# Gate and up chunks by seven products over all of K, interleaved with the down projection, in a two-layer encoder trunk

## The chip, the core and the metric

The kernel runs on one core of a Trainium2 chip. The metric is device time in microseconds (us) of one execution. TensorE (PE) multiplies, VectorE (DVE) and ScalarE (ACT) work on elements, GpSimd (POOL) and SyncE (SP) issue DMAs here, and 16 DMA engines carry the data. A trace is the record of one execution, every instruction with its start and duration.

## The reference

Two layers over 256 tokens of width 2048: an input projection, attention and retention heads, an output projection, then a gated feed-forward part, each followed by a layer norm. What matters here is the feed-forward part:

```
D_MODEL = 2048; SEQ = 256; DEPTH = 2
D_FF = -(-(8 * D_MODEL) // (3 * 256)) * 256          # 5632
...
f = (jax.nn.silu(x @ w_gate[l]) * (x @ w_up[l])) @ w_down[l]
x = layer_norm(ALPHA * x + f, ln2_g[l], ln2_b[l])
```

All of it is float32, and the weights are read once from the chip's memory (HBM).

## The kernel before

**Three products for one.** A float32 operand is split in two: `hi`, a copy rounded to the matmul's format (fp32r), and `lo`, what the copy left out. A product is then hi·hi + hi·lo + lo·hi, three TensorE instructions (lines 252 to 254, 819 to 821). `split` (L263) makes the two: ACT casts `hi` (L264), then DVE subtracts (L265).

**Weight units.** The weights come in units, in the order of the list `UNITS`. A plain unit (`std`) is one block of 512 rows and 512 columns, 128x2048 in the core's memory, 1 MB. The class `Weights` runs three steps ahead: `_load` issues the DMA on SP (L162), `_prep` splits a unit (L183 to L206), `get` hands it to the products, and `done` (L240) preps the unit three further on. There are three `hi` and three `lo` buffers. So the cast of a unit can't start until TensorE is done with the unit three before it.

**Chunks.** 11 chunks of 512 columns make up the 5632 columns of gate and up. Chunk 0 is plain. In chunks 1 to 10, gate and up of the same columns, two halves of the tokens and two blocks of rows form a 2 by 2 matrix product, done with seven block products in place of eight. The blocks are 11 and 21 (gate, upper and lower rows) and 12 and 22 (up). Three products take a block as it is (B11, B21, B22), four take a sum: T1 = 11 + 12, T2 = T1 + 22, T4 = T2 + 21, T3 = 12 + 22. T1, T2 and T4 are made in place in the buffer of block 11, so each sum waits until the unit before it in that buffer is split. Before, a sum is made by DVE (L201), only T3 by a DMA that adds as it writes (L199, issued by POOL). The matching forms of the input, s1 to s4, are made once per layer (`s_sums`, `s_turn`). This covers 1024 of the 2048 rows; the other rows run as four plain units (sg2, sg3, su2, su3: gate and up).

**Order.** A chunk's units are B11, sg2, T1, B21, T2, sg3, T3, T4, su2, B22, su3. A product of one form has 12 matmuls of 512 columns, a plain unit has 24. The products go to the banks X, Q, W, Y, Z and R of PSUM (the tiles sX, sQ, ...), and eight DVE steps of 512 columns and three ACT steps join them into h. `h_flush` transposes h and splits it for the down projection. After chunks 0 to 2, 3 to 5, 6 and 7, and 8 to 10 (`FF_PARTS`) the down projection runs over those chunks: one unit of 24 matmuls of 512 columns per chunk and per quarter of the 2048 output columns (banks db), then two adds to the residual (L707).

Tile, the layer in which the kernel is written, schedules each engine's instructions by its own cost model when the program is built. Every engine then runs its list in that order.

Of the kernel before, what the change touches and what calls it, by code (L numbers as in the profile page):

```python
# [10 lines left out]
F32 = mybir.dt.float32  # L11
# [17 lines left out]
FF_PARTS = ((0, 3), (3, 6), (6, 8), (8, 11))  # L29
STRASSEN_ADD_BY_DMA = ("T3",)  # L30
# [14 lines left out]
def weight_plan():  # L45
# [9 lines left out]
    def strassen(l, c):  # L55
        b = {}
        for i in ("11", "12", "22", "21"):
            b[i] = add("w_gate" if i[1] == "1" else "w_up", l, 512 * (int(i[0]) - 1), 4, 512 * c, 512)
        for kind in ("B11", "sg2", "T1", "B21", "T2", "sg3", "T3", "T4", "su2", "B22", "su3"):
            if kind[0] == "s":  # L60
                block("w_gate" if kind[1] == "g" else "w_up", l, 512 * int(kind[2]), 4, 512 * c, 512)
            else:
                units.append((kind, b))

    for l in range(DEPTH):
# [25 lines left out]
        for f0, f1 in FF_PARTS:  # L91
            for c in range(f0, f1):
                if c == 0:
                    for name in ("w_gate", "w_up"):
                        for u in range(4):
                            block(name, l, 512 * u, 4, 512 * c, 512)
                else:
                    strassen(l, c)
            for n in range(4):
                for c in range(f0, f1):  # L100
                    block("w_down", l, 512 * c, 4, 512 * n, 512)
# [6 lines left out]
def shift(b):  # L108
    name, _, _, _, c0, ncol = PLAN[b]
    if name == "w_in" and ncol == 128:  # L110
        return 16
    if name == "w_uq" and c0 < 1024 or name == "w_ukv" and c0 < 1024:
        return 48
    return 0
# [9 lines left out]
def trunk(ctx: ExitStack, tc: tile.TileContext, x, pos, w, lnp, cols, eye, consts, out):  # L124
# [26 lines left out]
    class Weights:  # L151
# [26 lines left out]
        def _prep(self):  # L178
# [7 lines left out]
            if kind == "std":  # L186
                n = SIZES[b]
                raw = self.raw.pop(b)
                o = shift(b)
                for a, e in ((0, n // 2), (n // 2, n)):  # L190
                    split(hi[:, o + a:o + e], lo[:, o + a:o + e], raw[:, a:e])
            else:
                r = {j: self.raw.get(b[j]) for j in b}
                into, frm = {"B11": ("11", None), "B21": ("21", None), "B22": ("22", None), "T1": ("11", "12"),
                             "T2": ("11", "22"), "T4": ("11", "21"), "T3": ("12", "22")}[kind]
                if frm is not None:
                    if kind in STRASSEN_ADD_BY_DMA:
                        j = b[frm]
                        G.dma_start(r[into], w[OFFS[j]:OFFS[j + 1]].rearrange("(p n) -> p n", p=P), accum_op=ALU.add)  # L199
                    else:  # L200
# [27 lines left out]
        def get(self, m=1):  # L228
            r = []
            for _ in range(m):  # L230
# [3 lines left out]
                n, ncol, o = (SIZES[b], PLAN[b][5], shift(b)) if kind == "std" else (2048, 512, 0)  # L234
# [200 lines left out]
    for l in range(DEPTH):  # L435
# [330 lines left out]
        def s_sums():  # L766
            x_ = lambda t, c: res[:, t, 512 * c:512 * (c + 1)]
            sforms.extend(vt512(f"sf{i}") for i in range(4))
            s1, s2, s3, s4 = sforms
            V.tensor_tensor(s1, x_(1, 0), x_(1, 1), ALU.subtract)  # L770
            V.tensor_tensor(s2, x_(0, 0), s1, ALU.subtract)
            V.tensor_tensor(s3, x_(1, 0), x_(0, 0), ALU.subtract)
            V.tensor_tensor(s4, x_(0, 1), s2, ALU.subtract)

        def s_turn(u):
            for i in ((), (0, 1), (2,), (3,))[u]:
                pt = bank("pts")
                for j in range(4):
                    PE.transpose(pt[:, j * P:(j + 1) * P], sforms[i][:, j * P:(j + 1) * P], ident)
                split(sfh[:, i, :, :], sfl[:, i, :, :], pt.rearrange("p (j t) -> p j t", j=4))  # L780

        hprev = []

        def h_flush(hTh, hTl, f0):
            while hprev:
                t, c, hh = hprev.pop(0)
# [3 lines left out]
                k0 = 4 * (c - f0)  # L790
                split(hTh[:, k0:k0 + 4, t * P:(t + 1) * P], hTl[:, k0:k0 + 4, t * P:(t + 1) * P],
                      pt.rearrange("p (j t) -> p j t", j=4))

        def plain_group(c, flush):
            gb = [bank(f"gb{t}") for t in range(2)]
            chunk_head(gb, 512, 4, xTh, xTl, s_sums)
# [5 lines left out]
            flush()  # L802
            ub = [bank(f"ub{t}") for t in range(2)]
            chunk_plain(ub, 512, 4, xTh, xTl, 0, then=s_turn)
            for t in range(2):
                V.tensor_tensor(sg[t], sg[t], ub[t], ALU.mult)
                hprev.append((t, c, sg[t]))

        def strassen_group(c, flush):
            x11 = (xTh[:, 0:4, 0:P], xTl[:, 0:4, 0:P])  # L810
            x12 = (xTh[:, 4:8, 0:P], xTl[:, 4:8, 0:P])
            x22 = (xTh[:, 4:8, P:S], xTl[:, 4:8, P:S])
            s1, s2, s3, s4 = ((sfh[:, i], sfl[:, i]) for i in range(4))

            def mm(ps, unit, st, first=False):
                wh, wl = unit
                for k in range(4):
                    a, b = st[0][:, k, :], st[1][:, k, :]
                    PE.matmul(ps, a, wh[:, k, :], start=first and k == 0, stop=False, skip_group_check=True)  # L819
                    PE.matmul(ps, a, wl[:, k, :], start=False, stop=False, skip_group_check=True)  # L820
                    PE.matmul(ps, b, wh[:, k, :], start=False, stop=k == 3, skip_group_check=True)  # L821

            def xs(t, u):
                return (xTh[:, 4 * u:4 * u + 4, t * P:(t + 1) * P], xTl[:, 4 * u:4 * u + 4, t * P:(t + 1) * P])

            bX = bank("sX")
            (unit,) = W.get()
            mm(bX, unit, x11, True)
            v2 = vt512("v2")
            A.copy(v2, bX)  # L830
            W.done()
            bQ = bank("sQ")
            (unit,) = W.get()
            mm(bQ, unit, xs(1, 2), True)
            mm(bX, unit, xs(0, 2))
            W.done()
            flush()
            bW = bank("sW")
            (unit,) = W.get()
            mm(bW, unit, s1, True)  # L840
            W.done()
            (unit,) = W.get()
            mm(bX, unit, x12)
            W.done()
            bY = bank("sY")
            (unit,) = W.get()
            mm(bY, unit, s2, True)
            V.tensor_tensor(v2, bY, v2, ALU.subtract)
            W.done()
            (unit,) = W.get()  # L850
            mm(bX, unit, xs(0, 3))
            sg = vt512("sg")
            A.activation(sg, bX, AF.Silu)
            mm(bQ, unit, xs(1, 3))
            W.done()
            bZ = bank("sZ")
            (unit,) = W.get()
            mm(bZ, unit, s3, True)
            v3, v5 = vt512("v3"), vt512("v5")
            V.tensor_tensor(v3, bZ, v2, ALU.add)  # L860
            V.tensor_tensor(v5, bW, v3, ALU.add)
            W.done()
            (unit,) = W.get()
            mm(bQ, unit, x22)
            V.tensor_tensor(v3, bQ, v3, ALU.subtract)
            A.activation(v3, v3, AF.Silu)
            W.done()
            bR = bank("sR")
            (unit,) = W.get()
            mm(bR, unit, xs(1, 2), True)  # L870
            mm(bW, unit, xs(0, 2))
            W.done()
            (unit,) = W.get()
            mm(bW, unit, s4)
            W.done()
            (unit,) = W.get()
            mm(bW, unit, xs(0, 3))
            V.tensor_tensor(v2, bW, v2, ALU.add)
            V.tensor_tensor(v2, v2, sg, ALU.mult)
            mm(bR, unit, xs(1, 3))  # L880
            V.tensor_tensor(v5, bR, v5, ALU.add)
            V.tensor_tensor(v5, v5, v3, ALU.mult)
            W.done()
            hprev.append((0, c, v2))
            hprev.append((1, c, v5))
# [139 lines left out]
```

## Time and profile before

| | |
|---|---|
| device time, median of 3 | 2193.23 us (2192.56 to 2194.4) |
| the profiled execution's own time | 2195.18 us |
| its span, first to last instruction | 2193.4 us |
| TensorE busy | 2160.7 us (99%) |
| VectorE, ScalarE busy | 1590.7 us (73%), 1025.1 us (47%) |
| mean granted TensorE clock | 0.997 of full speed |

Busy time of an engine is the union of its instructions' spans. Matmuls overlap in the pipeline, so what one costs is the distance from its start to the next one's start, and not its duration in a row. The view of waits names, for each pause of an engine, who ended it.

### The profile page before, as it was taken

What the parts mean: (1) busy time and instruction counts of PE and PEld (TensorE: products, weight loads), DVE (VectorE), ACT (ScalarE), POOL (GpSimd) and SP (SyncE); (2) the same over time, 40 slices, a digit from 0 to 9 for tenths busy, and PEclk for the clock granted to TensorE, in tenths of its full rate; (3) what the DMA queues carried; (4) which work ended last, traced back from release to release, by engine and by line L of the source; (5) the groups of instructions that cost most, each with busy time, mean ns of one, the idle gap of its engine ahead of it and who ended that gap; (6) DMA issues with size and microseconds to landing.
All of it is one profiled execution on the core that took longest, in us unless ns stands there. A gap on an engine that the chain in (4) does not pass through costs nothing. (4 is left out here: it accounts for less than half of the span.)

```text
span 2193.4 us, 26857 instructions
## 1 busy us (share of the span) xinstructions
PE 2160.7 (99%) x11084; PEld 1839.4 (84%) x11084; DVE 1590.7 (73%) x1695; ACT 1025.1 (47%) x1089; POOL 35.5 (2%) x46
## 2 busy tenths in 40 slices
PE   7999999999999999999999999999999999999998
PEld 5988988788888888888889899878888888888886
DVE  8565675887698578788675656667966885877976
ACT  4554333555455345455344543335544553545552
POOL 0000000000000000000000000000000000000000
PEclk9999999999999999999999999999999999999999
DMA  7544555566567557475555444555665765666653
GB/s 258 208 156 152 175 194 190 211 211 230 173 224 257 206 196 245 163 254 203 189 185 184 154 156 172 211 192 192 219 241 177 246 235 173 206 249 211 211 211 115
DMA packets 63467, 440.70 MB, mean 201 GB/s; under 512 B 7408, under 2 KB 7664, under 8 KB 11504
## 3 DMA queue, kind: packets, MB, share of 16 engines
q1 hardware_dynamic: 60320, 417.94, 52.3%
q0 software_dynamic: 2880, 20.97, 5.2%
q8 instruction: 87, 1.43, 0.3%
q14 instruction: 36, 0.29, 0.0%
q10 hardware_dynamic: 144, 0.07, 0.0%
HBM read 436.85 MB, written 2.10 MB: 200 GB/s over the span
## 5 line engine op out<-in xcount | busy, mean ns | idle before, releaser
L264 ACT CAST hi<-raw 128x1024 fp32r<-128x1024 f32 (+3 forms) x754 | 875.5, 1201 | 981.1 <-PE db L254 294.0
L265 DVE TENSOR_TENSOR lo<-raw,hi 128x1024 fp32r<-128x1024 f32 (+3 forms) x754 | 1033.5, 1407 | 410.6 <-ACT hi L264 408.8
L252 PE MATMUL db<-hi,hTh 128*128 128x512 f32 x704 | 276.0, 392 | 0.0
L253 PE MATMUL db<-lo,hTh 128*128 128x512 f32 x704 | 274.1, 389 | 0.0
L254 PE MATMUL db<-hi,hTl 128*128 128x512 f32 x704 | 271.5, 389 | 0.0
L252 PEld LDWEIGHTS db<-hi,hTh 128*128 128x128 f32 x704 | 132.2, 188 | 30.1 <-ACT hTh L264 3.8
L254 PEld LDWEIGHTS db<-hi,hTl 128*128 128x128 f32 x704 | 132.1, 188 | 28.0
L253 PEld LDWEIGHTS db<-lo,hTh 128*128 128x128 f32 x704 | 132.2, 188 | 26.6
L259 PE MATMUL prq<-xTh,hi 128*128 128x256 f32 x512 | 144.3, 282 | 0.0
L260 PE MATMUL prq<-xTl,hi 128*128 128x256 f32 x512 | 142.9, 279 | 0.0
L261 PE MATMUL prq<-xTh,lo 128*128 128x256 f32 x512 | 142.9, 279 | 0.0
L201 DVE TENSOR_TENSOR raw<-raw,raw 128x2048 f32<-128x2048 f32 x60 | 137.1, 2286 | 0.5
L821 PE MATMUL sX<-hi,xTl 128*128 128x512 f32 x320 | 124.5, 389 | 0.0
L819 PE MATMUL sX<-hi,xTh 128*128 128x512 f32 x320 | 124.5, 389 | 0.0
L820 PE MATMUL sX<-lo,xTh 128*128 128x512 f32 x320 | 124.5, 389 | 0.0
L259 PEld LDWEIGHTS prq<-xTh,hi 128*128 128x128 f32 x512 | 97.4, 190 | 0.1
L260 PEld LDWEIGHTS prq<-xTl,hi 128*128 128x128 f32 x512 | 96.2, 188 | 0.1
L261 PEld LDWEIGHTS prq<-xTh,lo 128*128 128x128 f32 x512 | 96.1, 188 | 0.0
L819 PE MATMUL sQ<-hi,xTh 128*128 128x512 f32 x240 | 93.4, 389 | 0.0
L820 PE MATMUL sQ<-lo,xTh 128*128 128x512 f32 x240 | 93.4, 389 | 0.0
L821 PE MATMUL sQ<-hi,xTl 128*128 128x512 f32 x240 | 93.4, 389 | 0.0
L707 DVE SCALAR_TENSOR_TENSOR res<-res,db 128x512 f32<-128x512 f32 x64 | 43.8, 684 | 66.0 <-PE db L254 66.0
(266 smaller groups left out, 3973.7 us busy)
## 6 DMA issues: line engine op xcount, KB each, us to landing
raw<-w SPq DMA_DIRECT2D x377, 1024.0 KB, 4.9
raw<-w POOLq DMA_DIRECT2D x20, 1024.0 KB, 8.6
raw<-w SPq DMA_DIRECT2D x8, 640.0 KB, 3.8
lng<-lnp SPq DMA_DIRECT2D x4, 1024.0 KB, 4.7
lnb<-lnp SPq DMA_DIRECT2D x4, 1024.0 KB, 5.7
res<-x SPq DMA_DIRECT2D x4, 512.0 KB, 6.3
out<-res SPq DMA_DIRECT2D x8, 256.0 KB, 2.3
cst<-consts SPq DMA_DIRECT2D x2, 720.5 KB, 7.7
```

The lines of the kernel that those rows point to most:

```text
L201: V.tensor_tensor(r[into], r[into], r[frm], ALU.add)
L252: PE.matmul(ps[:, :ncol], sh, wh[:, k, :ncol], start=first and k == 0, stop=False)
L253: PE.matmul(ps[:, :ncol], sh, wl[:, k, :ncol], start=False, stop=False)
L254: PE.matmul(ps[:, :ncol], sl, wh[:, k, :ncol], start=False, stop=last and k == nk - 1)
L259: PE.matmul(ps_ap, wh[:, k, c0:c0 + P], xh[:, k, :], start=k == 0, stop=False)
L260: PE.matmul(ps_ap, wh[:, k, c0:c0 + P], xl[:, k, :], start=False, stop=False)
L261: PE.matmul(ps_ap, wl[:, k, c0:c0 + P], xh[:, k, :], start=False, stop=k == nk - 1)
L264: A.copy(hi, src)
L265: V.tensor_tensor(lo, src, hi.bitcast(F32), ALU.subtract)
L819: PE.matmul(ps, a, wh[:, k, :], start=first and k == 0, stop=False, skip_group_check=True)
L820: PE.matmul(ps, a, wl[:, k, :], start=False, stop=False, skip_group_check=True)
L821: PE.matmul(ps, b, wh[:, k, :], start=False, stop=k == 3, skip_group_check=True)
```

## The change

Chunks 2, 4, 6, 8 and 10 take their seven products over all 2048 rows, with no plain units: each is done twice, for 256 columns at a time, with 8 row tiles of 256 columns per block (24 matmuls of 256 columns per product). T1 and T2 are made by DVE, T3 and T4 by the adding DMA. Chunks 1, 3, 5, 7 and 9 stay as they were in arithmetic, with a new order, and T3 by DVE and T4 by DMA. The down projection's units (D in the list below) of the two chunks before are placed between the products of each full chunk: four per half in chunks 2, 4, 6 and 8, two per half in chunk 10. What is left (eight units) runs at the end. The forms s1 to s4 now cover all of the input, so there are two sets.

```diff
-FF_PARTS = ((0, 3), (3, 6), (6, 8), (8, 11))
-STRASSEN_ADD_BY_DMA = ("T3",)
+HALF_ORDER = ("B11", "T1", "sg1", "T2", "B21", "sg3", "T3", "su1", "B22", "su3", "T4")
+FULL_ORDER = {4: ("B11", "T1", "T2", "D", "B21", "D", "T3", "D", "B22", "D", "T4"),
+              2: ("B11", "T1", "T2", "B21", "D", "T3", "B22", "D", "T4")}
+FF_STEPS = [("half", 1, ())]
+for _f in (2, 4, 6, 8):
+    FF_STEPS += [("full", _f, tuple((n, (_f - 2, _f - 1)) for n in range(4))), ("half", _f + 1, ())]
+FF_STEPS += [("full", 10, ((0, (8, 9)), (1, (8, 9))))]
+FF_LAST = ((2, (8, 9, 10)), (0, (10,)), (1, (10,)), (3, (8, 9, 10)))
+ADD_BY_DMA = {512: ("T4",), 256: ("T3", "T4")}
...
-                if frm is not None:
-                    if kind in STRASSEN_ADD_BY_DMA:
-                        j = b[frm]
-                        G.dma_start(r[into], w[OFFS[j]:OFFS[j + 1]].rearrange("(p n) -> p n", p=P), accum_op=ALU.add)
-                    else:
-                        V.tensor_tensor(r[into], r[into], r[frm], ALU.add)
-                split(hi[:, :2048], lo[:, :2048], r[into])
-                for j in {"T4": ("11", "21"), "T3": ("12",), "B22": ("22",)}.get(kind, ()):
+                if frm is not None and kind not in by_dma:
+                    V.tensor_tensor(r[into], r[into], r[frm], ALU.add)
+                split(hi[:, o:o + 2048], lo[:, o:o + 2048], r[into])
+                nxt = {"T1": ("T3", "12", "22"), "T2": ("T4", "11", "21")}.get(kind)
+                if nxt is not None and nxt[0] in by_dma:
+                    j = b[nxt[2]]
+                    G.dma_start(r[nxt[1]], w[OFFS[j]:OFFS[j + 1]].rearrange("(p n) -> p n", p=P), accum_op=ALU.add)
+                for j in {"T4": ("11",), "T3": ("12",), "B22": ("22",), "B21": ("21",)}.get(kind, ()):
...
+            for i, kind in enumerate(order):
+                if kind == "D":
+                    next(downs)()
+                    continue
+                (unit,) = W.get()
+                if kind == "B11":
+                    acc("X", unit, xs(0, 0, nk))
+                    A.copy(v2, B["X"])
+                elif kind == "T1":
+                    acc("W", unit, s1)
+                elif kind == "T2":
+                    acc("Y", unit, s2)
+                    V.tensor_tensor(v2, B["Y"], v2, ALU.subtract)
...
+                elif kind == "T4":
+                    acc("Q", unit, xs(1, 8, nk))
+                    V.tensor_tensor(v3, B["Q"], v3, ALU.subtract)
+                    A.activation(v3, v3, AF.Silu)
+                    V.tensor_tensor(v5, v5, v3, ALU.mult)
...
+                W.done()
+                if i == 1:
+                    flush()
```

The order of the built programs at the place on which the most rests. A number behind a tile's name is that of the unit or the buffer; `hi84` and `lo84` are the halves of unit 84.

**VectorE at the start of a chunk, before.** Chunk 2 of layer 0: unit 80 is B11, 82 T1, 83 B21, 84 T2, and `raw77` is the buffer of block 11, so the two L201 rows make T1 and T2. L878 to L882 finish chunk 1.

```order
L201 TENSOR_TENSOR raw77_4025<-raw77_4025,raw78_4070 128x2048
L879 TENSOR_TENSOR v2_3884<-v2_3884,sg_4005 128x512
L881 TENSOR_TENSOR v5_4041<-sR_4072,v5_4041 128x512
L882 TENSOR_TENSOR v5_4041<-v5_4041,v3_4040 128x512
L265 TENSOR_TENSOR lo82_4152<-raw77_4025,hi82_4151 128x2048
L265 TENSOR_TENSOR lo83_4174<-raw80_4101,hi83_4173 128x2048
L201 TENSOR_TENSOR raw77_4025<-raw77_4025,raw79_4121 128x2048
L265 TENSOR_TENSOR hTl_3517<-pth_4207,hTh_3516 128x4x128
L265 TENSOR_TENSOR hTl_3517<-pth_4214,hTh_3516 128x4x128
L265 TENSOR_TENSOR lo84_4203<-raw77_4025,hi84_4202 128x2048
```

And after, at the start of the second half of chunk 2: unit 91 is B11, 92 T1, 93 T2, and `raw85` is the buffer of block 11. L731 adds a down projection's result to the residual, L916 and L918 finish the half before.

```order
L289 TENSOR_TENSOR lo91_4499<-raw85_4403,hi91_4498 128x2048
L731 SCALAR_TENSOR_TENSOR res_71<-res_71,db0_4440 128x512
L220 TENSOR_TENSOR raw85_4403<-raw85_4403,raw86_4438 128x2048
L731 SCALAR_TENSOR_TENSOR res_71<-res_71,db1_4441 128x512
L916 TENSOR_TENSOR v3_4196<-sQ_4538,v3_4196 128x256
L289 TENSOR_TENSOR lo92_4531<-raw85_4403,hi92_4530 128x2048
L918 TENSOR_TENSOR v5_4197<-v5_4197,v3_4196 128x256
L220 TENSOR_TENSOR raw85_4403<-raw85_4403,raw87_4470 128x2048
L289 TENSOR_TENSOR lo93_4567<-raw85_4403,hi93_4566 128x2048
```

The lo of B21 stood between T1's lo and T2's sum and is gone from there; a residual add stands ahead of T1's sum now.

**TensorE around T2's product, before**, in the same chunk: unit 83 (B21) goes before it.

```order
L820 MATMUL sX_4158<-lo83_4174,xTh_72 128x512
L821 MATMUL sX_4158<-hi83_4173,xTl_73 128x512
L819 MATMUL sY_4259<-hi84_4202,sfh_3514 128x512
L820 MATMUL sY_4259<-lo84_4203,sfh_3514 128x512
L821 MATMUL sY_4259<-hi84_4202,sfl_3515 128x512
```

And after, at the second half of chunk 2, where unit 94 is a down projection's:

```order
L874 MATMUL sW_4606<-lo92_4531,sfh_3514 128x256
L875 MATMUL sW_4606<-hi92_4530,sfl_3515 128x256
L873 MATMUL sY_4637<-hi93_4566,sfh_3514 128x256
L276 MATMUL db0_4669<-hi94_4600,hTh0_3948 128x512
L276 MATMUL db1_4670<-hi94_4600,hTh0_3948 128x512
L874 MATMUL sY_4637<-lo93_4567,sfh_3514 128x256
L875 MATMUL sY_4637<-hi93_4566,sfl_3515 128x256
```

T2's product (sY) follows T1's (sW) at once, and two matmuls of the unit behind it are drawn in between its first and its second.

## Rows read from the trace of the kernel before

**Rows 1.** The page's first part: busy us (share of the span) xinstructions

```profile
PE 2160.7 (99%) x11084; PEld 1839.4 (84%) x11084; DVE 1590.7 (73%) x1695; ACT 1025.1 (47%) x1089; POOL 35.5 (2%) x46
```

**Rows 2.** Stretch of chunks 1, 2: us; busy PE, PEld, DVE, ACT, POOL; PEclk, DMA, GB/s

```profile
441.70:525.10 83.40, 83.40 (x377) 69.14 (x376) 72.85 (x55) 47.97 (x41) 0.88 (x1) 1.00 0.69 237
```

**Rows 3.** Timeline of TensorE: start us, us, what; 512 columns, 12 matmuls apart

```profile
547.29 0.39 PE L252 MATMUL db<-hi,hTh 128*128 128x512 f32 x1
...
550.01 0.39 PE L252 MATMUL db<-hi,hTh 128*128 128x512 f32 x1
```

**Rows 4.** The same for 256 columns, 42 matmuls apart

```profile
100.05 0.28 PE L261 MATMUL pg<-xTh,lo 128*128 128x256 f32 x1
...
105.00 0.28 PE L261 MATMUL pg<-xTh,lo 128*128 128x256 f32 x1
```

**Rows 5.** Groups of the page: busy us, mean ns | idle; weight loads of 256-column matmuls

```profile
L259 PEld LDWEIGHTS prq<-xTh,hi 128*128 128x128 f32 x512 | 97.4, 190 | 0.1
```

**Rows 6.** Timeline of TensorE, eight transposes and what follows

```profile
491.58 1.03 PE L789 MATMUL pth<-ident,v 128*128 128x128 f32 x8
492.37 0.48 PE L819 MATMUL sW<-hi,sfh 128*128 128x512 f32 x1
```

**Rows 7.** Groups by shape, whole span: busy us, mean ns | idle before, releasers

```profile
L265 DVE TENSOR_TENSOR lo<-raw,hi 128x2048 fp32r<-128x2048 f32 x140 | 320.2, 2287 | 94.1 <-ACT hi L264 92.6
L264 ACT CAST hi<-raw 128x2048 fp32r<-128x2048 f32 x140 | 268.1, 1915 | 241.6 <-DVE raw L201 104.5 <-PE db L254 41.5 <-PE sW L821 31.4
L201 DVE TENSOR_TENSOR raw<-raw,raw 128x2048 f32<-128x2048 f32 x60 | 137.1, 2286 | 0.5
L707 DVE SCALAR_TENSOR_TENSOR res<-res,db 128x512 f32<-128x512 f32 x64 | 43.8, 684 | 66.0 <-PE db L254 66.0
```

**Rows 8.** Timeline of VectorE, the start of chunk 2

```profile
482.52 2.28 DVE L201 TENSOR_TENSOR raw<-raw,raw 128x2048 f32<-128x2048 f32 x1
...
491.36 2.28 DVE L201 TENSOR_TENSOR raw<-raw,raw 128x2048 f32<-128x2048 f32 x1
...
495.68 4.56 DVE L265 TENSOR_TENSOR lo<-raw,hi 128x2048 fp32r<-128x2048 f32 x3 [0.83 <-ACT hi L264]
```

**Rows 9.** Timeline of ScalarE, the same stretch

```profile
484.91 1.92 ACT L264 CAST hi<-raw 128x2048 fp32r<-128x2048 f32 x1 [4.69 <-DVE raw L201]
...
493.73 3.81 ACT L264 CAST hi<-raw 128x2048 fp32r<-128x2048 f32 x3 [0.45 <-DVE raw L201]
```

**Rows 10.** Timeline of TensorE where T2's product begins

```profile
497.68 0.39 PE L821 MATMUL sX<-hi,xTl 128*128 128x512 f32 x1
497.90 0.39 PE L819 MATMUL sY<-hi,sfh 128*128 128x512 f32 x1
```

**Rows 11.** Timelines: a product's last matmul, and ScalarE's step that waits for it

```profile
444.18 0.39 PE L821 MATMUL sX<-hi,xTl 128*128 128x512 f32 x1
...
444.61 0.59 ACT L830 COPY v<-sX 128x512 f32<-128x512 f32 x1 [0.76 <-PE sX L821]
```

**Rows 12.** Timeline of VectorE: steps of 256 columns in a row

```profile
300.26 0.42 DVE L638 TENSOR_TENSOR rqkt<-ra,rb 128x256 f32<-128x256 f32 x1
300.60 0.42 DVE L639 TENSOR_TENSOR rqkt<-ra,rb 128x256 f32<-128x256 f32 x1
```

**Rows 13.** Stretches at the start of layer 1, columns as in Rows 2

```profile
1108.00:1110.00 2.00, 1.35 (x4) 0.78 (x5) 2.00 (x6) 0.56 (x1) 0.92 (x1) 0.97 0.05 13
1110.00:1112.00 2.00, 2.00 (x8) 1.66 (x7) 1.31 (x2) 0.48 (x1) 0.00 (x0) 0.50 0.00 0
1112.00:1114.00 2.00, 2.00 (x8) 1.53 (x8) 1.86 (x3) 0.11 (x1) 0.00 (x0) 0.68 0.00 0
```

**Rows 14.** DMA issues: count, KB each, median us to landing

```profile
raw<-w SPq DMA_DIRECT2D x377, 1024.0 KB, 4.9
raw<-w POOLq DMA_DIRECT2D x20, 1024.0 KB, 8.6
```

**Rows 15.** DMAs of the tile raw

```profile
DMA to landing us min/median/max: 3.5/4.9/10.9
```

More of the change, by code (lines that the diff above doesn't have):

```diff
@@ L53, in block, with std, down, strassen @@
         units.append(("std", add(*a)))
[L55 to L61, printed above, removed]
-            else:
-                units.append((kind, b))
+    def std(l, key, c):
+        block("w_gate" if key[1] == "g" else "w_up", l, 512 * int(key[2]), 4, 512 * c, 512)
+    def down(l, n, c):
+        block("w_down", l, 512 * c, 4, 512 * n, 512)
+    def strassen(l, c, half=None):
+        rows, nk, c0, ncol = (1024, 4, 512 * c, 512) if half is None else (1024, 8, 512 * c + 256 * half, 256)
+        return {i: add("w_gate" if i[1] == "1" else "w_up", l, rows * (int(i[0]) - 1), nk, c0, ncol)
+                for i in ("11", "12", "22", "21")}
     for l in range(DEPTH):
@@ L90, in weight_plan @@
                 block("w_out", l, 512 * u, 4, 512 * c, 512)
[L91 to L101, printed above, removed]
+        for name in ("w_gate", "w_up"):
+            for u in range(4):
+                block(name, l, 512 * u, 4, 0, 512)
+        for mode, c, groups in FF_STEPS:
+            if mode == "half":
+                b = strassen(l, c)
+                for kind in HALF_ORDER:
+                    if kind[0] == "s":
+                        std(l, kind, c)
+                    else:
+                        units.append((kind, b))
+            else:
+                todo = [(n, cc) for n, cs in groups for cc in cs]
+                per = len(todo) // 2
+                for half in range(2):
+                    b = strassen(l, c, half)
+                    for kind in FULL_ORDER[per]:
+                        if kind == "D":
+                            down(l, *todo.pop(0))
+                        else:
+                            units.append((kind, b))
+        for n, cs in FF_LAST:
+            for c in cs:
+                down(l, n, c)
     return plan, units
@@ L109, in shift @@
     name, _, _, _, c0, ncol = PLAN[b]
-    if name == "w_in" and ncol == 128:
-        return 16
-    if name == "w_uq" and c0 < 1024 or name == "w_ukv" and c0 < 1024:
-        return 48
+    if name in ("w_gate", "w_up") and ncol == 256:
+        return 48
+    if name == "w_in" and ncol == 128 or name in ("w_uq", "w_ukv") and c0 < 1024:
+        return 16
     return 0
@@ L801, in plain_group, with turns @@
                 sg.append(s_)
-            flush()
             ub = [bank(f"ub{t}") for t in range(2)]
-            chunk_plain(ub, 512, 4, xTh, xTl, 0, then=s_turn)
+            def turns(u):
+                if u == 1:
+                    s_turn(0)
+                    s_sums(1)
+                if u == 3:
+                    s_turn(1)
+            chunk_plain(ub, 512, 4, xTh, xTl, 0, then=turns)
             for t in range(2):
                 V.tensor_tensor(sg[t], sg[t], ub[t], ALU.mult)
-                hprev.append((t, c, sg[t]))
@@ L809, in strassen_group @@
[L809 to L885, printed above, removed]
@@ new lines, in plain_group, with xs, mm @@
+            hprev.append((0, sg))
+        def xs(t, k0, nk):
+            ts = slice(t * P, (t + 1) * P)
+            return (xTh[:, k0:k0 + nk, ts], xTl[:, k0:k0 + nk, ts])
+        def mm(ps, unit, st, first=False):
+            wh, wl = unit
+            nk = st[0].shape[1]
+            for k in range(nk):
+                a, b = st[0][:, k, :], st[1][:, k, :]
+                PE.matmul(ps, a, wh[:, k, :], start=first and k == 0, stop=False, skip_group_check=True)
+                PE.matmul(ps, a, wl[:, k, :], start=False, stop=False, skip_group_check=True)
+                PE.matmul(ps, b, wh[:, k, :], start=False, stop=k == nk - 1, skip_group_check=True)
@@ new lines, in trunk @@
+        plain_group()
+        for mode, c, groups in FF_STEPS:
+            v = [vt512(n) for n in ("v2", "v3", "v5", "sg")]
+            if mode == "half":
+                strassen_group(HALF_ORDER, 4, 512, 0, v, None)
+            else:
+                downs = down_list(groups)
+                per = sum(len(cs) for _, cs in groups) // 2
+                for half in range(2):
+                    strassen_group(FULL_ORDER[per], 8, 256, 256 * half, v, downs)
+            hprev.append((c, (v[0], v[2])))
@@ new lines, in trunk @@
+        g, b = ln_params(ffp, ("sfh", "sfl"), 2 + 2 * l)
+        for i, d in enumerate(down_list(FF_LAST[:-1], normf)):
+            d()
+            if i == 0:
+                flush()
+        last = l == DEPTH - 1
+        n, cs = FF_LAST[-1]
+        db3 = [bank(f"db{t}") for t in range(2)]
+        units = W.get(3)
+        for t in range(2):
+            for i, c in enumerate(cs):
+                mm_x(db3[t], 512, t, units[i], *hT[c], 0, 4, i == 0, i == 2)
+                if t:
+                    W.done()
+                    if i < 2:
+                        pop(1)
+            resid(db3, n, t, normf, 1.0)
+            normf.close(t)
+            for cc in range(4):
+                if last:
+                    normf.apply(t, cc, g, b, transpose=False)
+                    nc.sync.dma_start(out[t * P:(t + 1) * P, 512 * cc:512 * (cc + 1)],
+                                      res[:, t, 512 * cc:512 * (cc + 1)])
+                else:
+                    pend.append(lambda t=t, cc=cc: normf.apply(t, cc, g, b))
```

141 lines of the change are left out of this document (82 added, 59 removed).

## The prediction

> **What bounds the kernel now.** I read the page's first part first: TensorE is busy for 99% of the span, VectorE for 73% [rows 1]. Next, the busy time by stretch: in chunks 1 and 2 TensorE pauses nowhere (83.40 of 83.40 us), and VectorE is at 72.85 us, 87%, so it has little room [rows 2]. Then the timelines, for the price of a matmul: 512 columns take (550.01 - 547.29) / 12 = 0.2267 us from start to start [rows 3], 256 columns (105.00 - 100.05) / 42 = 0.1179 us [rows 4]. So TensorE sets the time, work taken from it counts in full, and any pause given to it counts too. How near the pauses are shows at the start of chunk 2. VectorE makes T2's sum at 491.36, ScalarE casts it from 493.73, VectorE's lo begins at 495.68 and ends 2.29 later, at 497.97 [rows 7 to 9]. TensorE begins T2's product at 497.90 and needs the lo for its second matmul, at 498.13 [rows 3, 10]. The order before meets T2 with under 0.2 us to spare.
>
> **The products.** A chunk by the old form has 7 x 12 + 4 x 24 = 180 matmuls of 512 columns: 180 x 0.2267 = 40.8 us. By the new form it has 2 x 7 x 24 = 336 of 256: 336 x 0.1179 = 39.6 us. That is 1.2 us less per chunk, for 10 full chunks in two layers **-12.0 us**. Of the 12.5% that seven for eight saves on the other half of the rows, the narrower matmul gives most back. The down projection has as many matmuls as before.
>
> The new set of s forms adds 16 transposes per layer, 32 x (492.37 - 491.58) / 8 = 32 x 0.099 = **+3.2 us** [rows 6]. Their splits and sums, the 24 more residual adds (0.68 us each [rows 7]) and the three more units to split per full chunk lie on VectorE and ScalarE beside TensorE, and cost nothing as an average. In one half of a full chunk VectorE has 7 lo (2.29 each), 2 sums (2.29), 4 lo of the down projection in two parts (about 2.3), 4 residual adds, and 7 steps of 256 columns (0.42): some 36 us [rows 7, 12], beside 7 x 2.83 + 4 x 5.44 = 41.6 us of TensorE. The cover is there on average. Whether it is there at each point is the question.
>
> **The start of a half.** The new order puts B11, T1, T2 in a row, each 24 x 0.1179 = 2.83 us on TensorE, and T1 and T2 are sums in one buffer. I count from the moment E at which TensorE ends B22 of the half before. Only then is the hi buffer for the next B11 free, since there are three. TensorE goes on with D (24 x 0.2267 = 5.44), T4, B11, T1 and comes to T2 at E + 5.44 + 3 x 2.83 = E + 13.9.
>
> The other two engines, for the second half of a chunk:
> - B11: ScalarE starts 0.20 after TensorE hands over (444.61 against 444.18 + 0.23 [rows 3, 11]), casts 1.92, to 2.1. VectorE does two steps of the half before until 2.3 (0.34 from one to the next [rows 12]), then lo 2.29: to 4.6.
> - T1: the residual add that stands ahead of it in VectorE's order (0.6), to 5.1; the sum 2.29, to 7.4; the cast 0.11 later (484.91 against 482.52 + 2.28 [rows 8, 9]), to 9.4; the lo, to 11.8.
> - T2: its sum overwrites what T1's lo reads, so it waits for that and one step: 12.0 to 14.3; cast, 14.4 to 16.3; lo, 16.4 to 18.7.
>
> TensorE stands at T2's second matmul with its queue in order: behind it are the rest of T2, the down projection's unit and B21, and ScalarE's next casts wait for their buffers. It has one matmul of T2 and two of the down projection to fill in (0.12 + 0.45). So it loses 18.7 - 13.9 - 0.6 = **4.2 us**, first at T1 (about 0.5), most at T2. This is not made good later: TensorE is the bound, and the next half counts from its own E.
>
> The first half of a full chunk starts after su3 and T4 of a half-row chunk. The old chunk's steps have 512 columns (0.69 in place of 0.42), and h's split stands ahead of T2's lo. By the same walk T4's lo ends at 1.7, B11's at 4.9, T1's sum at 7.8, its cast at 9.8, its lo at 12.1, T2's sum at 14.9, its cast at 17.0 and its lo at E + 19.3. TensorE gets there at 4.53 (what is left of su3) + 2.72 + 2 x 2.83 + 0.8 (eight transposes) = 13.7, and loses **5.0 us**. In chunk 10 D comes later in the order, and the residual add ahead of T1's sum waits for it: the second half loses 5.4. At the start of chunks 3, 5, 7 and 9 sg1 (5.44 us) stands between T1 and T2, but VectorE makes T3's sum between T1's sum and T1's lo. T1's sum ends at 7.4, T3's at 10.1, T1's lo at 12.3 (TensorE fills the time with transposes and single matmuls and waits 0.1), T2's sum at 17.5, its cast at 19.6, B21's cast, of which one matmul is drawn ahead, at 21.5, T2's lo at 21.9. TensorE, there at 20.3, waits 1.4 more: 1.5 us. For chunk 1 and the tail I take nothing.
>
> Sum: 10 x 5.0 + 8 x 4.2 + 2 x 5.4 + 8 x 1.5 = **+106.4 us**. Its lower bound is the chain with nothing else on VectorE: 3 x 2.29 for the lo, 2 x 2.29 for the sums, 3 x 1.92, 0.2 + 2 x 0.11 + 3 x 0.04, some 17.8, less 13.9 and 0.6: 3.3 us at 20 places, 66. Upward it is bounded by a DMA that is late (below).
>
> **The clock.** At the start of layer 1 TensorE, waiting for transposes, was busy for 1.35 of 2 us; its granted clock then fell from 2.4 GHz to 1.2 for the next 3 us (0.97, 0.50, 0.68 of full speed in three stretches of 2 us), which cost (0.03 + 0.50 + 0.32) x 2 = 1.7 us [rows 13]. The new pauses are longer than that one, and lie in 20 places. Each costs between 0 and 1.7 us; the only pause in the rows that is like them fell, so I take a value towards the upper end, 1.2: **+24 us**. By the rule of the Trainium skill (TensorE: Matmul & The Clock Gate, "HAM oscillation — how this bites in real kernels") a loop that leaves TensorE waiting in each tile pays for the drop in each tile and not once; by it the sum has up to 20 x 1.7 = 34 us here, without it 0. The one drop in the rows agrees with it as far as it goes.
>
> **The DMAs.** A half of a full chunk loads 8 blocks and adds 2 more, 10 x 1.05 MB in 45 us, 235 GB/s, as in the stretch of chunks 1 and 2 (237 GB/s) [rows 2]. T3's and T4's adding DMAs are issued when T1's sum and T2's lo are done and land 8.6 us later [rows 14], with over 15 us until TensorE wants them. The block 22 of the next half is issued when T4's lo is done, at E + 1.6, and wanted at 7.5 (T3's sum, chunks 3, 5, 7, 9) or at 12: at 4.9 us to landing [rows 14] it is in time, at 10.9, the longest [rows 15], chunks 3 to 9 would lose up to 5 us each, 38 in 8 places. I take 0.
>
> **Sum.** 2195.18 (the profiled execution's own time) - 12.0 + 3.2 + 106.4 + 24 = 2316.8. The profiled execution lies 0.09% above the median of the runs, 2193.23; against that the forecast is 2193.2 + 121.6, **2315 us**, 5.5% slower. What measurement can tell from no change is about 0.2%.
>
> **Rivals.**
> - The pauses come as worked out but the clock stays at 2.4 GHz: 2315 - 24 = 2291. For it: a few matmuls run inside each pause. Against: so they did before the drop in the rows.
> - Block 22 comes late (above): 2315 + 38 = 2353. For it: four loads are in the air together, and the loads of a half wait in SP's order behind T4's lo. Against: the longest landing in the rows is not the usual one.
> - Faster: VectorE gets ahead and keeps ahead, because its load is some 36 of 41.6 us in each half, so that T2 is ready when TensorE comes. The place is the start of a half, the price is that the 106 and the 24 go: 2193.2 - 12.0 + 3.2 = 2184. It decides once the chain from E to T2's lo is shorter than 14.5 us. For it: before, TensorE never paused [rows 2]. Against: getting ahead takes a free hi buffer, and the shortest chain that the rows allow is 17.8; before, sg2 and B21 stood around T1, 5.44 + 2.72 us more for the same chain, and it fitted by 0.2 us.
> - The 256-column matmuls wait for their weight loads, 190 ns each [rows 5]: 336 x 0.190 = 63.8 us a chunk, 23.0 more than before, 230 in all; TensorE then comes to T2 at E + 5.44 + 3 x 4.56 = 19.1, and the chain fits: 2193 + 230 + 3 + 12 = 2438. The rows speak against it: the same loads stand behind matmuls that follow each other in 118 ns [rows 4, 5]. By the Trainium skill (TensorE: Matmul & The Clock Gate, "Part 3: Packing small matmuls — row/col tiling", on the mechanism) a weight load overlaps with a matmul in flight only when it goes to other rows of the array, which would give this time; the trace shows the overlap with full 128-row loads.
>
> **How the numbers follow.** The forecast's case, pauses and some clock, has 0.56; pauses without the clock 0.20; late loads 0.11; T2 in time 0.05; weight loads 0.02; the rest, 0.06, is spread around the pauses' lower bound, 2193.2 - 8.8 + 66 = 2250 without a clock term. The range goes from 2258, just above that bound, to 2350, just under the late loads in full: the first case and the second lie inside whole, and about 2 in 10 is left out. Faster by over 0.2%: 0.05, the one case that gives it. Within 0.2%: 0.02, a half-way form of that case. Slower: 0.93.
>
> **What would show it.** In the profile after: 256-column products 0.118 us apart inside a product; at the start of each half of chunks 2 to 10 a pause of TensorE before T2's (sY's) second matmul, 4 us with its small parts, ended by DVE lo (L289), and behind it the clock at 0.5 for some us; TensorE's busy share down to about 95%; ScalarE's waits for the sums (L220) up. It is wrong if sY's second matmul waits under 1 us, if the pauses end on a DMA, or if they lie at D or T3.

## The result and the profile after

The changed kernel takes 2328.1 us (median of 4 runs, 2325.7 to 2334.2), the kernel before 2192.9 us beside it: 1.062 times as long, 95% interval 1.0599 to 1.0642, 135 us more. The forecast was 2315 us, the range 2258 to 2350. The profiled execution has 2328.0 us and a span of 2326.2. The kernel before, run again beside each set of experiments, took 2194.4 us beside e1 to e4, 2193.1 beside e5 to e8 and 2192.9 beside e9 and e10, so a difference between two sets is sure only to 1 or 2 us.

From the page of the changed kernel, the busy time of the engines (us, share of the span, instructions), and the shares of the chain of work that ended last (in the last line those of the kernel before):

```profile
PE 2208.3 (95%) x12676; PEld 1929.0 (83%) x12676; DVE 1696.3 (73%) x1795; ACT 1082.2 (47%) x1117; POOL 61.7 (3%) x76
PE 38%; DVE 7%; ACT 3%; issue 2%; DMA 0%; DVEq 0%; ACTq 0%
PE 48%; DVE 1%; issue 0%; ACT 0%; DVEq 0%; ACTq 0%
```

TensorE's busy share fell from 99% [rows 1] to 95%, although it has less to compute, and VectorE and ScalarE now stand in the chain, with 7% and 3% in place of 1% and 0%. The waits of TensorE in the changed kernel (us in total, times, longest; sW is T1's bank, sY T2's, sX B11's and B21's):

```profile
PE sY L873 <- ACT hi L288: 30.6, 20, 1.6
PE sW L874 <- DVE lo L289: 20.7, 21, 1.8
...
PE sX L873 <- ACT hi L288: 11.2, 12, 1.4
PE sY L874 <- DVE lo L289: 9.8, 16, 0.7
PE db L276 <- ACT hi L288: 9.0, 16, 0.6
PE sR L874 <- DVE lo L289: 4.0, 10, 0.4
```

T2's product waits 20 times for its cast, once in each half of each full chunk of two layers, and 16 times for its lo behind that. The view puts most of the idle time on the cast, since T2's first matmul waits for it; the last to come is the lo. No wait of TensorE ends on a DMA; the loads land in 5.5 us and the adding DMAs in 8.9, against 4.9 and 8.6 [rows 14]. One load was late, in chunk 3 of layer 1, where T3's sum on VectorE waited for it:

```profile
1730.50 2.29 DVE L220 TENSOR_TENSOR raw<-raw,raw 128x2048 f32<-128x2048 f32 x1 [0.86 <-DMA raw<-w]
```

Now one such place, the start of the second half of chunk 4 in layer 0. TensorE's last matmul of B22 before it begins at 665.29, the next unit at 665.41; this is the E of the prediction. VectorE's timeline (start, length, operation; in square brackets the idle time ahead of it and what ended that):

```profile
667.72 2.28 DVE L289 TENSOR_TENSOR lo<-raw,hi 128x2048 fp32r<-128x2048 f32 x1
669.92 0.68 DVE L731 SCALAR_TENSOR_TENSOR res<-res,db 128x512 f32<-128x512 f32 x1
670.52 2.28 DVE L220 TENSOR_TENSOR raw<-raw,raw 128x2048 f32<-128x2048 f32 x1
...
674.85 2.29 DVE L289 TENSOR_TENSOR lo<-raw,hi 128x2048 fp32r<-128x2048 f32 x1 [0.55 <-ACT hi L288]
677.06 0.42 DVE L918 TENSOR_TENSOR v<-v,v 128x256 f32<-128x256 f32 x1
677.39 2.28 DVE L220 TENSOR_TENSOR raw<-raw,raw 128x2048 f32<-128x2048 f32 x1
681.70 6.76 DVE L289 TENSOR_TENSOR lo<-raw,hi 128x2048 fp32r<-128x2048 f32 x4 [2.02 <-ACT hi L288]
```

B11's lo, T1's sum, T1's lo, T2's sum, and the first lo of the last row, T2's, in a chain. T2's lo ends at 681.70 + 2.29 = 683.99, E + 18.6. TensorE's timeline at the same place:

```profile
677.20 0.39 PE L874 MATMUL sW<-lo,sfh 128*128 128x256 f32 x1 [0.41 <-DVE lo L289]
...
679.82 0.28 PE L875 MATMUL sW<-hi,sfl 128*128 128x256 f32 x1
681.72 0.38 PE L873 MATMUL sY<-hi,sfh 128*128 128x256 f32 x1 [1.62 <-ACT hi L288]
682.67 1.22 PE L276 MATMUL db<-hi,hTh 128*128 128x512 f32 x2 [0.57 <-ACT hi L288]
684.05 0.58 PE L874 MATMUL sY<-lo,sfh 128*128 128x256 f32 x1 [0.16 <-DVE lo L289]
684.43 0.41 PE L875 MATMUL sY<-hi,sfl 128*128 128x256 f32 x1
684.64 0.41 PE L873 MATMUL sY<-hi,sfh 128*128 128x256 f32 x1
684.85 0.41 PE L874 MATMUL sY<-lo,sfh 128*128 128x256 f32 x1
```

TensorE is through with T1 at 679.93 and makes three matmuls, worth 0.57 us, until T2's second one at 684.05: 3.55 us are lost here, and some 0.6 at T1, of which its row shows 0.41 as idle. The matmuls behind it come 0.21 us apart instead of 0.118 [rows 4]. The stretches of 4 us around it show why (busy us of the engines in their usual order, then the granted clock, the DMA share, GB/s):

```profile
676.00:680.00 4.00, 3.59 (x30) 3.28 (x28) 3.68 (x3) 0.60 (x2) 0.00 (x0) 1.00 1.01 203
680.00:684.00 4.00, 1.70 (x4) 0.69 (x3) 2.30 (x2) 4.00 (x4) 0.00 (x0) 0.80 0.13 27
684.00:688.00 4.00, 3.95 (x18) 3.96 (x19) 4.00 (x3) 1.36 (x1) 0.88 (x1) 0.50 0.56 78
688.00:692.00 4.00, 4.00 (x20) 3.49 (x19) 2.44 (x4) 2.00 (x2) 0.00 (x0) 0.84 1.01 238
```

TensorE was busy for 1.70 of 4 us; the granted clock fell to 1.2 GHz, and the three stretches behind the first lack 0.80 + 2.00 + 0.64 = 3.4 us of full speed, some 7 us at half the clock.

### The profile page after: what moved, and what is told of

It is laid out like the page before. It is cut to its first block, busy times and chain, and to the rows that moved or that the text cites. A ratio compares the mean times of both kernels' runs of the same rounds, so it can differ in the third digit from the quotient of the medians.

```text
span 2326.2 us, 30343 instructions
## 1 busy us (share of the span) xinstructions
PE 2208.3 (95%) x12676; PEld 1929.0 (83%) x12676; DVE 1696.3 (73%) x1795; ACT 1082.2 (47%) x1117; POOL 61.7 (3%) x76
## 4 chain that ended last, share of the span: by engine, by line
PE 38%; DVE 7%; ACT 3%; issue 2%; DMA 0%; DVEq 0%; ACTq 0%
DVE lo L289 3%; PE db L278 3%; PE db L277 3%; PE db L276 3%; ACT hi L288 3%; DVE raw L220 2%; PE prq L284 1%; PE prq L283 1%; PE prq L285 1%; PE sX L873 1%; PE sX L874 1%; PE sX L875 1%; PE wo L278 1%; PE wo L276 1%; PE wo L277 1%
## 5 line engine op out<-in xcount | busy, mean ns | idle before, releaser
L289 DVE TENSOR_TENSOR lo<-raw,hi 128x1024 fp32r<-128x1024 f32 (+3 forms) x744 | 1098.1, 1509 | 465.7 <-ACT hi L288 464.9
L873 PE MATMUL sX<-hi,xTh 128*128 128x256 f32 (+1 forms) x480 | 155.4, 324 | 11.2 <-ACT hi L288 11.2
L874 PE MATMUL sX<-lo,xTh 128*128 128x256 f32 (+1 forms) x480 | 153.3, 319 | 0.0
L875 PE MATMUL sX<-hi,xTl 128*128 128x256 f32 (+1 forms) x480 | 152.5, 318 | 0.0
L874 PE MATMUL sW<-lo,sfh 128*128 128x256 f32 (+1 forms) x400 | 123.4, 308 | 20.7 <-DVE lo L289 20.7
L873 PE MATMUL sW<-hi,sfh 128*128 128x256 f32 (+1 forms) x400 | 121.0, 302 | 0.0
L875 PE MATMUL sW<-hi,sfl 128*128 128x256 f32 (+1 forms) x400 | 120.5, 301 | 0.0
L873 PEld LDWEIGHTS sX<-hi,xTh 128*128 128x128 f32 x480 | 90.7, 189 | 22.0 <-ACT hi L288 15.4
L873 PE MATMUL sY<-hi,sfh 128*128 128x256 f32 (+1 forms) x200 | 74.3, 372 | 30.6 <-ACT hi L288 30.6
L874 PEld LDWEIGHTS sW<-lo,sfh 128*128 128x128 f32 x400 | 75.2, 188 | 31.2 <-DVE lo L289 27.7
```

Of the source, the lines that this page charges most:

```text
L289: V.tensor_tensor(lo, src, hi.bitcast(F32), ALU.subtract)
L875: PE.matmul(ps, b, wh[:, k, :], start=False, stop=k == nk - 1, skip_group_check=True)
```

## The experiments

The theory under test: the row B11, T1, T2 makes TensorE wait for VectorE's sums and splits, and the wait drops the clock. The rival: the form itself costs (256-column matmuls, more DMA, more work on VectorE as an average).

**e1, the order in full chunks alone.**

```
-FULL_ORDER = {4: ("B11", "T1", "T2", "D", "B21", "D", "T3", "D", "B22", "D", "T4"),
-              2: ("B11", "T1", "T2", "B21", "D", "T3", "B22", "D", "T4")}
+FULL_ORDER = {4: ("B11", "D", "T1", "B21", "D", "T2", "D", "T3", "B22", "D", "T4"),
+              2: ("B11", "D", "T1", "B21", "T2", "T3", "D", "B22", "T4")}
...
                 if kind == "D":
                     next(downs)()
+                    if i == 1:
+                        flush()
```

The last two lines keep the transposes of the chunk before behind the second unit, which is a D now.

> The changed kernel with another order inside full chunks alone: units of the down projection stand between B11 and T1 and between T1 and T2, B21 ahead of T2. Same products, same DMAs. Theory (the row of sums T1, T2 behind B11 makes TensorE wait, and the wait drops the clock): the second matmul of T2's product no longer waits for VectorE's lo in full chunks, the clock stays at about 1.0 there; left are some 1.2 to 1.5 us at half-row chunks 3, 5, 7, 9: 2193 - 12.0 + 3.2 + 12, about 2200 us (2190 to 2225). Rival (256-column matmuls, or the greater load of VectorE and of the DMAs as an average, make the time): the order changes little, 2300 or more.

2222.6 us, 1.0128 of before (1.0113 to 1.0143). The same instructions in another order take 105 us less, so the rival is out. It is 22 us over the number taken, so something was left. Part of that lies at the starts of chunks 3, 5, 7 and 9, where a wait came that the changed kernel does not have: sg1's first matmul adds into bank X and waits until ScalarE has copied B11's product out of it.

```profile
PE sX L873 <- ACT v L897: 7.4, 8, 0.9
```

**e2, the half-row order too.**

```
-HALF_ORDER = ("B11", "T1", "sg1", "T2", "B21", "sg3", "T3", "su1", "B22", "su3", "T4")
+HALF_ORDER = ("B11", "sg1", "T1", "B21", "T2", "sg3", "T3", "su1", "B22", "su3", "T4")
```

> As e1, and in the half-row chunks too the units are moved: B11, sg1, T1, B21, T2, sg3, T3, su1, B22, su3, T4. Theory: the last waits at the starts of chunks 3, 5, 7 and 9 go as well, 2193 - 12.0 + 3.2, about 2185 us, 0.4% under the kernel before (2178 to 2200). Rival: an average load of VectorE is the cause, and this is no better than e1; or the order makes half-row chunks, which waited little, wait anew: above e1.

2210.2 us, 1.0073 (1.0056 to 1.0090). The step from e1, 12.4 us, has the size forecast for the starts of chunks 3, 5, 7 and 9, but in part by luck: e1 has the wait for bank X there, and e2 still has one of 0.4 us for T2's lo (below). The time is 25 us over 2185. Its trace has pauses at three kinds of place. One is chunk 10, here its second half in layer 0:

```profile
1035.34 0.39 PE L874 MATMUL sW<-lo,sfh 128*128 128x256 f32 x1 [1.32 <-DVE lo L289]
1041.76 0.38 PE L873 MATMUL sY<-hi,sfh 128*128 128x256 f32 x1 [0.81 <-ACT hi L288]
1043.55 0.58 PE L873 MATMUL sZ<-hi,sfh 128*128 128x256 f32 x1 [1.41 <-ACT hi L288]
```

T1, T2 and T3 wait there. Each half has two units of the down projection there and not four; that this is the reason is argued, not tried. The other two are the start of eight half-row chunks (T2's bank, sY), and a wait in each half-row chunk (sR, ten times, as in the changed kernel); see e7 to e10.

```profile
PE sR L874 <- DVE lo L289: 4.0, 10, 0.4
PE sY L874 <- DVE lo L289: 3.2, 8, 0.4
```

**e3, one unit moved.**

```
-FULL_ORDER = {4: ("B11", "T1", "T2", "D", "B21", "D", "T3", "D", "B22", "D", "T4"),
-              2: ("B11", "T1", "T2", "B21", "D", "T3", "B22", "D", "T4")}
+FULL_ORDER = {4: ("B11", "T1", "D", "T2", "B21", "D", "T3", "D", "B22", "D", "T4"),
+              2: ("B11", "T1", "D", "T2", "B21", "T3", "B22", "D", "T4")}
```

> The changed kernel with one unit of the down projection moved: in full chunks D stands between T1 and T2 in place of behind T2, and all else is as it was. Theory: TensorE then comes to T2 5.4 us later, at E + 19.4, and T2's lo is done at 18.7 to 19.3; left are the half us at T1 and up to 1 at T2, 20 places, and 12 at half-row chunks, few drops of the clock: 2193 - 8.8 + 12 + 10 to 30, 2207 to 2230 us, 2220 taken. Rival (the wait has another cause, such as late blocks or the load of VectorE as a whole): the wait moves to another product and the time stays over 2280.

2239.2 us, 1.0205 (1.0189 to 1.0220): 89 us less for one unit of 5.4 us that stands ahead of T2 and not behind it (in chunk 10 ahead of B21 too). The longest waits of TensorE in the feed-forward part of its trace:

```profile
PE sW L874 <- DVE lo L289: 13.7, 12, 1.3
PE sX L873 <- ACT hi L288: 10.8, 17, 0.7
PE sR L874 <- DVE lo L289: 4.0, 10, 0.4
```

None is left at T2 (sY). Small ones stay at T1 and B21, and the time is 9 us over the top of what was expected. From one end of B22's product to the next, chunk 10's halves still lose 2.4 and 4.0 us against e6, the others 1.2 to 2.0.

**e4, the pause filled.** In each half of a full chunk, ahead of T2's product:

```
+NFILL = 14
...
+                if kind == "T2" and nk == 8:
+                    pd = bank("fill")
+                    for _ in range(NFILL):
+                        PE.matmul(pd, xTh[:, 0, 0:P], xTh[:, 0:2, :], start=True, stop=True)
```

> The changed kernel with 14 idle matmuls of 512 columns (3.2 us, into a spare bank, result unused) put on TensorE ahead of T2's product in each half of a full chunk, where it would wait: TensorE is kept busy in most of the pause, and the waits for VectorE stay. By the theory with a price for the clock (about 33 us of the added 133 is the drop of the clock behind the pauses): the idle matmuls cost little, since TensorE would have waited there, the clock stays near 1.0, and the time falls to about 2297 us (2290 to 2310). By the rival that the clock costs nothing beside the waits: 2328 or more, with no fall. If TensorE had not waited there at all, 20 x 3.2 = 63 us would come on top: 2390.

2297.4 us, 1.0472 (1.0456 to 1.0487): 30.7 us under the changed kernel, with 63 us of matmuls more, whose result is thrown away. The same place in its trace, second half of chunk 4:

```profile
675.10 2.90 PE L896 MATMUL fill<-xTh 128*128 128x512 f32 x12
677.83 0.28 PE L874 MATMUL sY<-hi,sfh 128*128 128x256 f32 x1
677.95 0.63 PE L277 MATMUL db<-hi,hTh 128*128 128x512 f32 x2
679.22 0.38 PE L875 MATMUL sY<-lo,sfh 128*128 128x256 f32 x1 [0.63 <-DVE lo L290]
679.44 0.28 PE L876 MATMUL sY<-hi,sfl 128*128 128x256 f32 x1
```

TensorE still stands until the lo comes, but the matmuls behind it are 0.11 us apart, not 0.21. The mean granted clock of the profiled execution is 0.997, against 0.983 in the changed kernel; it falls at one of the 20 places. The halves themselves keep their waits (the table of places below). So about 31 us of the 135 are the clock's alone.

**e5, chunk 10 by half rows again,** on top of e2.

```
-FF_STEPS += [("full", 10, ((0, (8, 9)), (1, (8, 9))))]
-FF_LAST = ((2, (8, 9, 10)), (0, (10,)), (1, (10,)), (3, (8, 9, 10)))
+FF_STEPS += [("half", 10, ())]
+FF_LAST = ((2, (8, 9, 10)), (0, (8, 9, 10)), (1, (8, 9, 10)), (3, (8, 9, 10)))
```

> The kernel of e2 with chunk 10 in the half-row form again (its down projection for chunks 8 and 9 goes behind it), so that four chunks of eleven take the full form. In e2's trace TensorE pauses 4.2 us in chunk 10 of a layer, loses 1.7 us to the clock there, and pauses nowhere else but 0.4 us in each half-row chunk. Theory (what e2 still loses lies in chunk 10, whose two units of the down projection per half leave too little between the sums): 2 x (4.2 + 1.7 + about 1 for matmuls that run slowly out of a pause) = 14 less, 2 x 1.2 + 2 x 0.4 more for the form: 2210 - 14 + 3 = 2199 us (2195 to 2204). Rival (every full chunk carries a cost that the pauses do not show): 2 fewer of 10 give a fifth of e2's distance from 2184, 2205 or, with the products' saving lost, 2207 and more.

2205.3 us, 1.0055 (1.0043 to 1.0068): only 5 us less, at the rival's number. This run does not tell whether chunk 10 matters; its half-row form brought waits of its own (sZ, for its cast, 2 times 1.5 us).

**e6, no sums in full chunks,** the changed kernel's full order and e2's half-row order.

```
-                if frm is not None and kind not in by_dma:
+                if frm is not None and kind not in by_dma and ncol == 512:
```

> The changed kernel's own order in full chunks (B11, T1, T2 in a row), with the half-row order of e2, and without VectorE's sums T1 and T2 in full chunks: their products use the block as it was loaded, which leaves this part of the computation out. Products, splits, transposes and DMAs are as in the changed kernel. Theory (the time of the chain from E to T2's lo is the cause; without the two sums it is 2 x 2.3 us and more shorter than 18.7, which is under TensorE's 13.9 + 0.6): the pauses and the drops of the clock go, left is the form itself, 2193 - 12.0 + 3.2 + 5 for the 0.4 us in each half-row chunk: 2189 us (2184 to 2196). Rival (256-column products, more DMA or ScalarE's casts cost by themselves): over 2205.

The kernel leaves T1's and T2's sums out in full chunks, so that it computes something else. 2191.3 us, 0.9993 (0.9984 to 1.0002). With the row B11, T1, T2 untouched but the chain without its two sums, every pause of full chunks is gone; of TensorE's waits in the feed-forward part only this one is left:

```profile
PE sR L874 <- DVE lo L289: 4.0, 10, 0.4
```

The 256-column form costs nothing by itself. What full chunks lose hangs on the sums, and by e1, which keeps them, on the place where they stand: it is the length of the chain that counts, and not the load of VectorE.

**e7 and e8, T3's sum of half-row chunks by an adding DMA,** on top of e5 and of e2.

```
-ADD_BY_DMA = {512: ("T4",), 256: ("T3", "T4")}
+ADD_BY_DMA = {512: ("T3", "T4"), 256: ("T3", "T4")}
```

> e5 with T3's sum of the half-row chunks made by an adding DMA in place of VectorE. Theory: the 0.4 us that TensorE waits for VectorE's lo in each half-row chunk goes with 2.3 us of VectorE's work ahead of it: about 6 us under e5, some 2193 us, no longer different from the kernel before. Rival: the adding DMA (8.7 us to landing) comes late for T3's product, 2.7 + 2.7 + 5.4 us after T1's split: 10 to 20 us over e5.

> e2 (five full chunks) with T3's sum of the half-row chunks made by an adding DMA. Theory as for e7: some 5 us under e2, about 2205 us. Rival: the DMA comes late, over 2215.

2196.9 us, 1.0017 (1.0008 to 1.0026), and 2203.4 us, 1.0046 (1.0033 to 1.0060): 8.3 and 6.8 less, near the numbers, but not through the wait named: what went is T2's wait of 0.4 us at the starts of eight half-row chunks, and in e7 chunk 10's at sZ. The wait at sR is still there, with 2.3 us less on VectorE. By the traces the first is worth 0.7 us at each of the eight places. e7's trace, VectorE and then TensorE in the half-row chunk 1:

```profile
469.08 2.29 DVE L289 TENSOR_TENSOR lo<-raw,hi 128x2048 fp32r<-128x2048 f32 x1 [2.99 <-ACT hi L288]
471.29 0.68 DVE L909 TENSOR_TENSOR v<-sZ,v 128x512 f32<-128x512 f32 x1
471.89 1.22 DVE L289 TENSOR_TENSOR lo<-raw,hi 128x1024 fp32r<-128x1024 f32 x1
473.02 0.69 DVE L910 TENSOR_TENSOR v<-sW,v 128x512 f32<-128x512 f32 x1
```

```profile
472.38 0.39 PE L873 MATMUL sR<-hi,xTh 128*128 128x512 f32 x1
473.16 0.50 PE L874 MATMUL sR<-lo,xTh 128*128 128x512 f32 x1 [0.40 <-DVE lo L289]
...
473.98 0.39 PE L873 MATMUL sW<-hi,xTh 128*128 128x512 f32 x1
```

su1's second product adds into the bank of T1 (sW), which VectorE reads last at 473.02, behind B22's lo, v3 and half of su3's lo. TensorE has drawn su3's first matmuls ahead and stands at their lo.

**e9 and e10, that read made earlier,** on top of e7 and e8.

```
                     V.tensor_tensor(v2, B["Y"], v2, ALU.subtract)
+                    if ncol == 512:
+                        V.tensor_tensor(v5, B["W"], v2, ALU.add)
...
-                    V.tensor_tensor(v5, B["W"], v3, ALU.add)
+                    if ncol == 512:
+                        V.tensor_tensor(v5, B["Z"], v5, ALU.add)
+                    else:
+                        V.tensor_tensor(v5, B["W"], v3, ALU.add)
```

> e7 with one sum of the half-row chunks taken apart: VectorE adds W's bank to v2 after T2 and Z's bank after T3, in place of W's bank to v3 after T3 (one step of 0.68 us more, the same result but for rounding). su1's second product adds into W's bank and can't start before VectorE has read it; in e7's trace that read (L910) comes 3.2 us after T3's last matmul, behind lo, v3 and half of another lo, and TensorE waits 0.4 us for the next lo and stands some 0.3 to 0.5 more around it, 12 times. Theory (this is what e7 loses against the form's own 2193.2 - 9.6 + 3.2 = 2187): 2196.9 - 12 x 0.75 = 2188 us (2185 to 2191), a little under the kernel before, 0.2%. Rival (the rest of e7's distance is spread over the full chunks): 2195 or more.

> e8, five full chunks, with the same sum taken apart as in e9. Theory: 10 x 0.75 us under e8, 2203.4 - 7.5 = 2196 us; chunk 10's pauses stay, so it is 8 over e9 though one more chunk a layer takes the cheaper form. Rival (chunk 10 costs no more than another full chunk): at or under e9.

e9: 2185.7 us, 0.9966 of before (0.9952 to 0.9979), 11.2 us under e7. From one B22 to the next the traces differ by 0.8 us for each half-row chunk, 9 us at 12 of them; the rest may be two drops of the clock, at 398 and 1112 us, which e7's trace has and e9's has not. e10: 2195.7 us, 1.0011 (1.0002 to 1.0019), 7.7 under e8, 0.77 at each of 10 places. Two more full chunks, one in each layer, make e10 10 us slower than e9, where the count of matmuls gives a gain of 2.4; so chunk 10 is not worth the full form in this order, as e2's trace said. In e9 (first line) TensorE is busy without a break from 442 to 1098 us, as in the kernel before (second line):

```profile
442.00:1098.00 656.00, 656.00 (x3587) 568.00 (x3585) 539.38 (x450) 353.20 (x303) 24.52 (x28) 1.00 0.75 243
442.00:1098.00 656.00, 656.00 (x2938) 542.06 (x2937) 506.19 (x413) 327.36 (x290) 8.79 (x10) 1.00 0.62 213
```

e9 is the fastest of all: four full chunks of eleven, the sums apart, 7 us or 0.34% under the kernel before.

## Why the prediction was right, and where its sizes were off

The mechanism is the one forecast. By terms, in us:

| term | forecast | measured | from |
|---|---|---|---|
| products and transposes | -8.8 | -1.8 together with the next | e6 against before |
| su1's wait for the bank of T1 | 0 | 7.7 | e8 - e10 |
| starts of chunks 3, 5, 7, 9 | 12 | 11.9 | e4 against e6, place by place |
| waits in full chunks | 94.4 | 94.9 | the same, less 1.7 for the one drop of the clock in e4 |
| clock | 24 | 30.7 | changed kernel - e4 |

The places one by one, from the last matmul of one B22 product to that of the next, in us over e6, which has none of these waits; e4 has the waits with the clock held up, the changed kernel has both. An example is the second half of chunk 4 in layer 0: 48.2 us in the changed kernel, 45.7 in e4, 41.6 in e6.

| stretch | places | forecast without clock | e4 | changed kernel |
|---|---|---|---|---|
| first half, chunks 2 to 8 | 8 | 5.0 | 4.9 to 5.0 | 4.9 to 7.7 |
| second half, chunks 2 to 8 | 8 | 4.2 | 4.2 | 5.6 to 6.6 |
| first half, chunk 10 | 2 | 5.0 | 5.4, 5.2 | 6.6, 6.4 |
| second half, chunk 10 | 2 | 5.4 | 7.5 (the clock fell), 5.8 | 8.5, 8.6 |
| start of chunks 3, 5, 7, 9 | 8 | 1.5 | 1.5 | 1.5, once 2.4 |

- **The products.** Right as far as it can be told: -8.8 + 7.7 = -1.1 beside the measured -1.8. In e9, with four full chunks a layer and no waits, the same count gives -9.6 + 3.2 = -6.4, and -7.2 was measured.
- **The starts of halves.** Right to some tenths of a us. The walk along the chain gave T2's lo at E + 18.7 and TensorE there at E + 13.9; the trace has 18.6 and 14.5. The three first halves that take 4.9 to 5.0 us in the changed kernel too are those after which the clock did not fall.
- **The clock.** Mis-sized: "Each costs between 0 and 1.7 us". In the trace of the changed kernel it falls at 17 of the 20 places, at 13 of them for 1.7 us below full speed and at 4 for 3.4, as in the stretch shown: 36 us in all. The part that lies inside a pause costs nothing: against e4 a short drop costs 1.2 to 1.6 us, and e4 gives 31 in all. The Trainium skill (TensorE: Matmul & The Clock Gate, "HAM oscillation — how this bites in real kernels") says that such a loop pays in every tile; 17 of the 20 places agree, three do not.
- **The cost that was missed.** "For chunk 1 and the tail I take nothing" should have been worked out for the half-row chunks as well: their new order puts su1 behind T3, and nothing in the walk asked when T1's bank is read. The old order had T4 between T3 and the plain unit, the new one has not. The 7.7 us are measured with T3's sum made by DMA; the idle time in the view, 0.4 us ten times, is the same in the changed kernel. With the 6.7 us missing from the clock they make up the 13 us between 2315 and 2328 to about 1 us. Both misses have the same sign, so the forecast did not come near by errors that cancel.
- **The DMAs.** 0 was near: no wait of TensorE ends on one. The late block of the rival did occur, at one of the eight places named, the start of chunk 3 in layer 1: T3's sum waited 0.86 us for it, and this start took 2.4 us in place of 1.5.
- **The rivals.** Late loads, weight loads and "faster" are out by the tables above. That the faster case was near shows in e9: the same form is quicker than before once T2 is ready when TensorE comes, at 2185.7. It has one full chunk a layer fewer than the 2184 of the rival, for which the count gives 2187.

That the chain starts at E because there are three hi buffers was argued, not tried: a fourth pair does not fit in the memory beside the other stages.

## What to carry to other kernels

When units of work are put in a row, walk the chain of the engines that prepare them from the moment a buffer comes free, and compare its end with the time at which the bound engine arrives; an engine with a quarter of its time free can still be late at one place of every tile. A unit that needs only its cast and lo, put between two that need a sum as well, can be worth more than the arithmetic that the change saves. Ask of every accumulation bank who still reads it when the next product wants to add into it.

## What the runs showed of the hardware

Adding 63 us of matmuls whose result is thrown away made a kernel 31 us faster: the granted clock stayed at 2.4 GHz at 19 of the 20 places, where it had fallen at 17. Behind a pause the loss came in two sizes, 1.7 and 3.4 us of full speed, and the length of the pause does not tell which: pauses of the same 3.55 us in second halves were followed by 3.4 at 681 us and by 1.7 at 540, 822 and 962, and one of 3.7 us, at 495, by none. These runs do not explain it. At 0.50 of the clock a 256-column matmul took 0.213 us, 1.8 times and not twice the 0.118 of full speed.
